# Dense products of the gate and the output projection listed behind the value projections in one sequence beside a recurrence, and the first chunk's operands in tiles of other pools

## The chip, the core and the metric

The kernel runs on one NeuronCore of a Trainium2 chip. The metric is device time in microseconds (us), the median of three executions. Next to the times there is one execution that was profiled; every duration below comes from that trace unless the text says otherwise. Engines: PE is the tensor engine (PEld its weight loads), DVE the vector engine, ACT the scalar engine, POOL GpSimd, SP the engine that only issues DMAs; ACT issues DMAs too.

## The reference, cut

A trunk of two layers on 512 positions of 1024 channels, each a mixer and a gated ConvFFN. The change lies in the second mixer, RWKV-7, whose core is a recurrence over positions, for 16 heads of 64 channels:

```python
def step(state, inp):
    r_t, w_t, k_t, v_t, a_t, b_t = inp
    sa = jnp.einsum('bhvk,bhk->bhv', state, a_t)
    state = (state * w_t[:, :, None, :]
             + sa[..., None] * b_t[:, :, None, :]
             + v_t[..., None] * k_t[:, :, None, :])
    y_t = jnp.einsum('bhvk,bhk->bhv', state, r_t)
...
r = xr @ w_r
k = xk @ w_k
v = xv @ w_v
g = jax.nn.sigmoid(xg @ g1) @ g2
...
return (y * g) @ w_o
```

## The kernel before, in words

Operands are stored transposed, channels on the 128 partitions and the 512 positions in the free dimension, so that a 1024-channel tensor is 8 tiles. Every dense product is done in float32r with both operands split into a high and a low part: three matmuls (lines 295, 296, 297, in the helper `mm3`) for each 128x128 block of weights. Such three are called a **set** below. Line 296 stands once in each set, so counting it counts sets.

The recurrence is done in chunks of 64 positions. First `pairs()` goes through the 8 tiles of channels (two heads each): decay, scaled operands, the products within a chunk. It writes three things to DRAM: `std` (for each group of four tiles and each chunk: the scaled operands and the masked products), `btd` and `vtd`. `invert(g)` inverts the 64x64 triangular blocks of group g (4 tiles): a long series of small DVE instructions on `pr` and `tt` (lines 964, 965), two DVE transposes (lines 970, 971), copies on ACT (975), and small matmuls (985, 988). Then `scan(g)` runs the 8 chunks of group g one after the other, 16 chunks in all, numbered 0 to 15 here (0 to 7 are group 0). One chunk is this chain:

1. PE: `us` and `e` from the chunk's operands `st` and values `vu` (lines 1105, 1109).
2. DVE copies `us` to `wt` (1107).
3. PE: the inverse `ti` times `wt` (1118).
4. DVE and ACT copy the result into `vu`, one head half each (1119, 1120).
5. PE: the new state from `vu` and `cbt` (1125), the rest of the output (1130).
6. DVE adds the decayed old state and writes it into `vu` of the next chunk (1128). ACT copies the output to `y` (1133).

Every second chunk is followed by `finish` (norm, transpose at line 1156, scale). `load(g, c)` fetches `st`, `vu` and `cbt` of a chunk through the SP queue (lines 1069, 1071, 1074), three buffers of each, in a pool `scan` that is opened when the pool of `pairs` is closed and takes its memory.

Beside this chain runs dense work, in generators that are advanced one step at a time: `projections()` (keys, then the values `v`; with each value tile four centring matmuls at line 784, one at 798, and the DMA of `vtd` at line 790), `gates()` (the product with g1, for each of eight channel tiles an operand made on ACT and DVE at lines 1010, 1011, 213, 214; then the product with g2 into `aux`, closed by line 1040), and `project()` (the output product `w_o`, added into `h` at line 1196). `weave` advances the chain and, after every step of it, the dense generator (`fill`) and the inversion (`side`) at the rates in the table `RATES`: the first number of an entry is steps of dense work for one step of the chain, the second a lag in steps, the third (0.5 where it is missing) steps of the inversion. The scheduler of the language then places each instruction in its engine's queue as early as its tiles and these marks allow; each engine works through its queue in order.

In the code before, `fill` is `projections()` alone until both `scan(0)` and the inversion of group 1 are emitted. What is left of it is then emitted at once, and only then `fill` becomes `gates()` followed by `project()`.

Of the kernel before, what the change touches and what calls it, by code (L numbers as in the profile page):

```python
# [12 lines left out]
F32 = mybir.dt.float32  # L13
# [7 lines left out]
P = 128  # L21
D = 1024
KT = 8
T = 512
# [4 lines left out]
GN_EPS = 64e-5  # L29
C1 = -0.5 * math.exp(-0.5)  # L30

RATES = ((1.9, 2), (1.9, 6, 2.2), (0.65, 2, 1), (0.9, 2), (2, 2), (0.7, 6, 2.2))
LEAD = 3
WB = 4
FIRST0, WAIT, STEPS = 1, 1, (2, 2, 2, 2, 2)
NKEY = 3
# [107 lines left out]
class Emit:  # L144
# [549 lines left out]
    def rwkv_main(self, r, ctx, gain):  # L694
# [10 lines left out]
        def tile_(shape, tag, bufs):  # L705
            return ep.tile(shape, F32, tag=tag, bufs=bufs, name=self.uid(tag))
# [354 lines left out]
        def load(g, c):  # L1061
            while 4 * g + 3 not in vdone:
                next(fill)
            ps = slice(4 * g, 4 * g + 4)
            st = tile_([P, 4 * 3 * P + P], "st", SCAN)
            bt, vu = tile_([P, 4, 2, C], "cbt", SCAN), tile_([P, 2, 4, C], "vu", SCAN)
            for hd in range(2):
                o = P * (1 - hd)
                nc.sync.dma_start(st[H[hd], o:o + 12 * P], std[g][c, H[hd]].rearrange("p i t -> p (i t)"))
# [9 lines left out]
        def scan(g, late=iter(())):  # L1079

            ih = [(i, hd) for i in range(4) for hd in range(2)]
            y = None

            for c in range(NCH):
                last = c == NCH - 1
                if (g, c) not in chunks:
                    load(g, c)
                st, bt, vu = chunks.pop((g, c))
                if (g, c) != (1, NCH - 1):
                    load(g + last, (c + 1) % NCH)  # L1090
                if c % 2 == 0:
                    y = tile_([P, 4, 2, C], "y", 3)
                us = self.acc("us").rearrange("p (a i f) -> p a i f", a=2, i=4)
                e = self.acc("e").rearrange("p (a i f) -> p a i f", a=2, i=4)

                def ar(i, hd, n):
                    o = P * (3 * i + 1 + hd) + n * C
                    return st[:, o:o + C]

                def pt(i, hd):  # L1100
                    o = P * (3 * i + 3 * (1 - hd)) + C
                    return st[H[hd], o:o + C]

                for i, hd in ih:
                    nc.tensor.matmul(us[H[hd], 0, i, :], ar(i, hd, 0), vu[:, hd, i, :], start=True, stop=True)
                wt = tile_([P, 4, C], "wt", 4)
                V.tensor_copy(wt, us[:, 0])
                for i, hd in ih:
                    nc.tensor.matmul(e[H[hd], 0, i, :], ar(i, hd, 1), vu[:, hd, i, :],
                                     start=i == 0, stop=False, skip_group_check=True)  # L1110
                if not last:
                    s0 = tile_([P, 4, C], "wt", 4)
                    for hd in range(2):
                        G.tensor_tensor(s0[H[hd]], vu[H[hd], hd], bc(gc[H[hd], 4 * g:4 * g + 4, c], C), ALU.mult)
                self.step(late)
                yield
                for i, hd in ih:
                    nc.tensor.matmul(us[H[hd], 1, i, :], ti[g][H[hd], i, c, :], wt[H[hd], i, :], start=True, stop=True)
# [55 lines left out]
        def project():  # L1174

            def load(g, m):
                return self.weights(A["wo"][m:m + 2, :, 512 * g:512 * g + 512].rearrange("m p c -> p m c"), lo_eng=G)

            ws = Ahead([lambda g=g, m=m: load(g, m) for g in range(2) for m in range(0, KT, 2)] + [self.prefetch])
            def back(m):  # L1180
                if m < KT:
                    nc.sync.dma_start(self.h[m], r.hd[m])

            for g in range(2):
                while g not in gated:
                    yield
                for m in range(KT):
                    if g == m == 0:
                        back(0)
                    if g == 0:  # L1190
                        back(m + 1)
                    if m % 2 == 0:
                        w = ws.take()
                    a = self.acc("mm")
                    yield from self.dense_steps(a, w, outs[g], c0=m % 2 * 512)
                    V.tensor_tensor(self.h[m], self.h[m], a, ALU.add)  # L1196
                    if g == 1:
                        self.absorb(m, gain)
# [7 lines left out]
        def until(gen, end):  # L1206
            for _ in gen:
                yield
                if end():
                    return  # L1210


        fill = projections()
        main = pairs()
        self.weave(until(main, lambda: 3 in done), None, fill, *RATES[0], ktiles=STEPS[0])
        inv = invert(0)
        for _ in take(inv, FIRST0):
            pass
        self.weave(until(main, lambda: KT - 2 in done), inv, fill, *RATES[1], ktiles=STEPS[1])
        self.weave(main, inv, fill, *RATES[5], ktiles=STEPS[1])  # L1220
        for _ in inv:
            pass
        ctx.close()
        ep = ctx.enter_context(tc.tile_pool(name="scan", bufs=1))
        inv = invert(1)
        gw = {}
        r.sg = [ep.tile([P, T], F32R, name=f"sg{i}") for i in range(3)]
        load(0, 0)
        next(inv)
        for _ in range(LEAD):  # L1230
            next(fill, None)
        self.weave(scan(0), inv, fill, *RATES[2], ktiles=STEPS[2])
        for _ in inv:
            pass
        for _ in fill:
            pass
        fill = itertools.chain(gates(), project())
        self.weave(scan(1, left.pop()), None, fill, *RATES[3], ktiles=STEPS[3])
        self.weave(left.pop(), None, fill, *RATES[4], ktiles=STEPS[4])
        for _ in fill:  # L1240
# [71 lines left out]
```

## Time and profile before

| | |
|---|---|
| median of 3 executions (lowest, highest) | 1329.78 us (1329.23, 1330.55) |
| the profiled execution's own time | 1334.18 us |
| its span, first to last instruction | 1332.4 us |
| PE busy | 1277.4 us (96%) |
| DVE busy | 853.5 us (64%) |
| ACT busy | 630.7 us (47%) |
| POOL busy | 142.1 us (11%) |
| mean granted clock of PE | 0.975 |

The profiled execution lies 4.40 us above the median. A matmul that waits in the pipeline counts as busy, so a busy PE is not PE at its peak; whether it works at full rate is seen in the granted clock and in the distance from one matmul's start to the next.

### The profile page before, as it was taken

Reading aid. Unit: us, or ns where it says so; the run is one execution under the profiler, and the core shown is the slowest. Engines: PE = TensorE matmul, PEld = TensorE weight load, DVE = VectorE, ACT = ScalarE, POOL = GpSimd, SP = SyncE. Lnnn points to the kernel's source line nnn. Section 1 sums busy time; section 2 is a strip of 40 time slices with the busy share of each in tenths; the row PEclk is TensorE's granted clock in tenths of the full one; section 3 lists DMA queues with packets and bytes.
Section 4 is the critical chain, followed back from the end, with each engine's and each line's share of the span. In section 5 each row is a group of like instructions: output and inputs, shape, how many; then the busy total and the mean of one; then the engine's idle time right before and its main releaser. Section 6 shows DMA issues by size and latency. Waiting matters only on the chain.

```text
span 1332.4 us, 19460 instructions
## 1 busy us (share of the span) xinstructions
PE 1277.4 (96%) x7578; PEld 1025.6 (77%) x7578; DVE 853.5 (64%) x1371; ACT 630.7 (47%) x1072; POOL 142.1 (11%) x148
## 2 busy tenths in 40 slices
PE   8999999999999999999999797799999999999996
PEld 6778888888888888677777666567888888888886
DVE  5565487887884444857788573576677777773223
ACT  5444365555553333656775443343554445452221
POOL 3100200000000001211210112123300000000001
PEclk9999999999999999999999887899999999999998
DMA  7232355555566653247778765683233333332322
GB/s 260 83 111 79 111 160 171 167 166 166 168 187 223 214 180 107 80 140 213 204 216 247 189 156 119 140 211 98 79 95 95 95 96 99 102 95 87 103 87 75
DMA packets 101100, 189.06 MB, mean 142 GB/s; under 512 B 16976, under 2 KB 48464, under 8 KB 101008
## 3 DMA queue, kind: packets, MB, share of 16 engines
q10 hardware_dynamic: 36592, 109.46, 27.1%
q1 hardware_dynamic: 64416, 78.36, 20.8%
q8 instruction: 59, 0.97, 0.3%
q14 instruction: 33, 0.27, 0.1%
HBM read 146.63 MB, written 41.16 MB: 141 GB/s over the span
## 4 chain that ended last, share of the span: by engine, by line
PE 76%; DVE 8%; DMA 4%; issue 3%; ACT 3%; POOL 1%; ACTq 0%; SPq 0%; DVEq 0%; POOLq 0%
PE mm L295 8%; PE mm L296 7%; PE mm L297 7%; PE aux L296 5%; PE aux L295 5%; PE aux L297 5%; PE us L295 5%; PE us L297 5%; PE us L296 5%; PE e L297 5%; PE e L296 5%; PE e L295 5%; DVE tt L965 1%; DVE pr L964 1%; PE e L1130 1%
## 5 line engine op out<-in xcount | busy, mean ns | idle before, releaser
L213 ACT CAST wh<-w 128x512 fp32r<-128x512 f32 x356 | 217.0, 612 | 386.4 <-PE mm L296 105.7
L214 DVE TENSOR_TENSOR wl<-w,wh 128x512 fp32r<-128x512 f32 x348 | 240.9, 693 | 180.0 <-ACT wh L213 178.6
L295 PE MATMUL mm<-mxh,wh 128*128 128x512 f32 (+1 forms) x384 | 157.4, 410 | 1.6 <-DVE h L1196 1.2
L297 PE MATMUL mm<-mxh,wl 128*128 128x512 f32 (+1 forms) x384 | 153.1, 399 | 0.4 <-DVE wl L214 0.3
L296 PE MATMUL mm<-mxl,wh 128*128 128x512 f32 (+1 forms) x384 | 152.2, 396 | 0.0
L322 POOL TENSOR_TENSOR ss<-ss,sq 128x512 f32<-128x512 f32 x30 | 41.9, 1397 | 776.5 <-issue 594.8
L518 ACT ACTIVATE cv<-z,par 128x512 f32<-128x512 f32 x88 | 71.7, 817 | 36.0 <-DVE z L516 35.9
L295 PEld LDWEIGHTS mm<-mxh,wh 128*128 128x128 f32 (+1 forms) x384 | 72.2, 188 | 20.6 <-issue 3.6
L297 PEld LDWEIGHTS mm<-mxh,wl 128*128 128x128 f32 (+1 forms) x384 | 72.3, 189 | 18.2 <-issue 0.9
L295 PE MATMUL e<-mxh,wh 128*128 128x512 f32 x216 | 84.5, 391 | 0.0
L296 PEld LDWEIGHTS mm<-mxl,wh 128*128 128x128 f32 (+1 forms) x384 | 72.6, 189 | 14.9 <-issue 0.7
L296 PE MATMUL e<-mxl,wh 128*128 128x512 f32 x216 | 84.1, 389 | 0.0
L297 PE MATMUL e<-mxh,wl 128*128 128x512 f32 x216 | 84.0, 389 | 0.0
L296 PE MATMUL aux<-mxl,wh 128*128 128x512 f32 x208 | 81.4, 391 | 2.7 <-POOL mxl L214 2.0
L295 PE MATMUL aux<-mxh,wh 128*128 128x512 f32 x208 | 81.5, 392 | 0.3 <-ACT mxh L213 0.3
L519 DVE SCALAR_TENSOR_TENSOR cv<-z,par,cv 128x512 f32<-128x512 f32 x88 | 66.1, 752 | 23.9 <-ACT cv L518 23.9
L295 PE MATMUL us<-mxh,wh 128*128 128x512 f32 x208 | 81.3, 391 | 0.0
L297 PE MATMUL aux<-mxh,wl 128*128 128x512 f32 x208 | 81.0, 389 | 0.0
L297 PE MATMUL us<-mxh,wl 128*128 128x512 f32 x208 | 81.0, 389 | 0.0
L296 PE MATMUL us<-mxl,wh 128*128 128x512 f32 x208 | 80.9, 389 | 0.0
L520 DVE SCALAR_TENSOR_TENSOR cv<-z,par,cv 128x512 f32<-128x512 f32 x88 | 66.0, 752 | 2.9
L296 PEld LDWEIGHTS aux<-mxl,wh 128*128 128x128 f32 x208 | 39.1, 188 | 12.3 <-POOL mxl L214 2.7
(1074 smaller groups left out, 2715.8 us busy)
## 6 DMA issues: line engine op xcount, KB each, us to landing
w<-in_wup ACTq DMA_DIRECT2D x88, 512.0 KB, 3.6
w<-in_wdn ACTq DMA_DIRECT2D x32, 512.0 KB, 3.6
st<-std SPq DMA_DIRECT2D x32, 384.0 KB, 5.8
std<-lq SPq DMA_DIRECT2D x32, 256.0 KB, 4.4
w<-in_wdn ACTq DMA_DIRECT2D x16, 384.0 KB, 3.2
w<-in_wsu ACTq DMA_DIRECT2D x8, 512.0 KB, 3.7
w<-in_wso ACTq DMA_DIRECT2D x8, 512.0 KB, 3.6
pw<-in_wk SPq DMA_DIRECT2D x16, 256.0 KB, 3.4
```

What stands on the lines that cost most here:

```text
L213: nc.scalar.copy(hi[r, :n], src)
L214: (lo_eng or nc.vector).tensor_tensor(lo[r, :n], src, hi[r, :n].bitcast(F32), ALU.subtract)
L295: mm(acc, wh, xh, start=first, stop=False)
L296: mm(acc, wh, xl, start=False, stop=False)
L297: mm(acc, wl, xh, start=False, stop=last)
L322: nc.gpsimd.tensor_tensor(self.ss, self.ss, self.sq, ALU.add)
L518: nc.scalar.activation(c, z[:, 2:], AF.Identity, scale=cw(2, i), bias=self.p("conv_b", l * 44 + i))
L519: nc.vector.scalar_tensor_tensor(c, z[:, 1:T + 1], cw(1, i), c, ALU.mult, ALU.add)
L520: nc.vector.scalar_tensor_tensor(c, z[:, 0:T], cw(0, i), c, ALU.mult, ALU.add)
L964: V.tensor_tensor(q, a, b, ALU.mult)
L965: V.tensor_tensor(tt[:, 0:nj, j + 1:32], tt[:, 0:nj, j + 1:32], q, ALU.add)
L1130: nc.tensor.matmul(e[H[hd], 0, i, :], pt(i, hd), vu[H[hd], hd, i, :], start=False, stop=True, skip_group_check=True)
```

## The change

Three things are edited.

- **The dense work is one sequence.** `fill` is `projections()`, `gates()` and `project()` chained, from the start. The emission of all that is left of `projections()` after `scan(0)` is gone. So gate work can stand beside the last chunks of group 0.
- **The rates.** `scan(0)` is woven at 0.62 in place of 0.65 steps, `scan(1)` at 0.85 in place of 0.9, and `LEAD`, the dense steps ahead of the first chunk, is 4 in place of 3.
- **The first chunk's load.** `load(0, 0)` is called before the last pair's products are woven instead of after the pools have changed. Its tiles therefore are not those of the pool `scan`: `st` are four tiles of the ring `mxh`/`mxl` (operands of dense products), `cbt` is the scratch tile `ss`, `vu` the scratch tile `rb`. It takes eight DMAs of 64x384 for `st` in place of two of 64x1536, so 11 DMAs in place of 5.

```diff
-RATES = ((1.9, 2), (1.9, 6, 2.2), (0.65, 2, 1), (0.9, 2), (2, 2), (0.7, 6, 2.2))
-LEAD = 3
+RATES = ((1.9, 2), (1.9, 6, 2.2), (0.62, 2, 1), (0.85, 2), (2, 2), (0.7, 6, 2.2))
+LEAD = 4
...
-            st = tile_([P, 4 * 3 * P + P], "st", SCAN)
-            bt, vu = tile_([P, 4, 2, C], "cbt", SCAN), tile_([P, 2, 4, C], "vu", SCAN)
-            for hd in range(2):
-                o = P * (1 - hd)
-                nc.sync.dma_start(st[H[hd], o:o + 12 * P], std[g][c, H[hd]].rearrange("p i t -> p (i t)"))
+            if g == c == 0:
+                st = [t for _ in range(2) for t in (self.xr.tile([P, T], F32, tag=tag, bufs=10, name=self.uid(tag))
+                                                    for tag in ("mxh", "mxl"))]
+                bt = scratch("ss").rearrange("p (i a f) -> p i a f", i=4, a=2)
+                vu = scratch("rb").rearrange("p (a i f) -> p a i f", a=2, i=4)
+                for i in range(4):
+                    for hd in range(2):
+                        o = P * (1 - hd)
+                        nc.sync.dma_start(st[i][H[hd], o:o + 3 * P], std[g][c, H[hd], i])
+            else:
+                t = tile_([P, 4 * 3 * P + P], "st", SCAN)
+                st = [t[:, 3 * P * i:3 * P * i + T] for i in range(4)]
...
-        fill = projections()
+        fill = itertools.chain(projections(), gates(), project())
+        gw = {}
...
+        load(0, 0)
         self.weave(main, inv, fill, *RATES[5], ktiles=STEPS[1])
...
-        load(0, 0)
         next(inv)
...
         for _ in inv:
             pass
-        for _ in fill:
-            pass
-        fill = itertools.chain(gates(), project())
         self.weave(scan(1, left.pop()), None, fill, *RATES[3], ktiles=STEPS[3])
```

Line numbers of the new code are 12 higher from `scan` on: 1117 for 1105, 1121 for 1109, 1119 for 1107, 1130 for 1118, 1131 and 1132 for 1119 and 1120, 1137 for 1125, 1142 for 1130, 1168 for 1156, 1081, 1083, 1086 for 1069, 1071, 1074.

What this does to the queues, at the three places on which the prediction rests. A row is line, operation, written tile, read tiles, shape, and a count where rows repeat; the number behind a tile's name tells its allocation.

**DVE at the start of `scan(0)`**, before. `pr`/`tt` are the inversion of group 1, `gwl` and `gw` the low parts of the g2 weights, `wt` is step 2 of chunk 0:

```order
L965 TENSOR_TENSOR tt_6678<-tt_6678,pr_6679 128x11x21
L214 TENSOR_TENSOR gwl_7641<-w_1431_7633,gwh_7640 128x512
L964 TENSOR_TENSOR pr_6679<-li_6677,tt_6678 128x240
L227 TENSOR_TENSOR gw_7636<-w_1431_7633,gw_7636 32x512
L965 TENSOR_TENSOR tt_6678<-tt_6678,pr_6679 128x12x20
L964 TENSOR_TENSOR pr_6679<-li_6677,tt_6678 128x247
L965 TENSOR_TENSOR tt_6678<-tt_6678,pr_6679 128x13x19
L1107 COPY wt_6741<-us_6731 128x256
```

and after:

```order
L965 TENSOR_TENSOR tt_6687<-tt_6687,pr_6688 128x8x24
L964 TENSOR_TENSOR pr_6688<-li_6686,tt_6687 128x207
L1119 COPY wt_6767<-us_6757 128x256
L965 TENSOR_TENSOR tt_6687<-tt_6687,pr_6688 128x9x23
L964 TENSOR_TENSOR pr_6688<-li_6686,tt_6687 128x220
L965 TENSOR_TENSOR tt_6687<-tt_6687,pr_6688 128x10x22
L1131 COPY rb_6572<-us_6757 64x256
L964 TENSOR_TENSOR pr_6688<-li_6686,tt_6687 128x231
L214 TENSOR_TENSOR gwl_7345<-w_1400_7337,gwh_7344 128x512
```

Chunk 0's first copy stands eleven rows earlier, behind the inversion's row of 128x207 and ahead of the g2 weights. On PE the same six dense matmuls stand ahead of chunk 0 in both.

**SP**, after. The rows with `ss` and `rb` are chunk 0's `cbt` and `vu`; the four with `std_4379` and `lq` are products of the last two pairs; `st_6748` begins chunk 1's load, at the place where chunk 0's load begins in the code before:

```order
L861 DMA std_4379<-ar_6245 64x8x128 x2
L1086 DMA ss_6571<-btd 128x512
L895 DMA std_4379<-lq_6270 64x4x256 x2
L790 DMA vtd<-vt_6302 128x8x64
L895 DMA std_4379<-lq_6329 64x4x256 x2
L906 DMA btd<-bt_6362 128x8x128
L790 DMA vtd<-vt_6443 128x8x64
L1083 DMA rb_6572<-vtd 64x256 x2
L895 DMA std_4379<-lq_6472 64x4x256 x2
L895 DMA std_4379<-lq_6596 64x4x256 x2
L906 DMA btd<-bt_6638 128x8x128
L790 DMA vtd<-vt_6696 128x8x64
```

The eight DMAs of chunk 0's `st` stand further up, among the writes of the fifth pair's products.

**PE in chunk 6**, before; lines 985 and 988 are the inversion of group 1, and no dense work stands in chunks 4 to 8:

```order
L1105 MATMUL us_7392<-vu_7228,st_7226 64x64 x7
L1109 MATMUL e_7393<-vu_7228,st_7226 64x64 x7
L988 MATMUL aux_7417<-li_7269,tt_7288 32x32 x32
L1118 MATMUL us_7392<-wt_7402,ti_4912 64x64 x8
L988 MATMUL aux_7468<-li_7269,tt_7288 32x32 x32
L1125 MATMUL us_7392<-vu_7228,cbt_7227 64x64 x8
L1130 MATMUL e_7393<-vu_7228,st_7226 64x64 x8
```

and after; `mm_7411` and `mm_7412` are the sums of the product with g1, `mxh_7416` and `mxl_7417` its first operand:

```order
L988 MATMUL aux_7460<-li_7284,tt_7297 32x32 x7
L295 MATMUL mm_7411<-mxh_7416,w_1404_7348 128x512
L295 MATMUL mm_7412<-mxh_7416,wh_7350 32x512
L988 MATMUL aux_7460<-li_7284,tt_7297 32x32 x6
L296 MATMUL mm_7411<-mxl_7417,w_1404_7348 128x512
L297 MATMUL mm_7411<-mxh_7416,w_1405_7349 128x512
L296 MATMUL mm_7412<-mxl_7417,wh_7350 32x512
L297 MATMUL mm_7412<-mxh_7416,wl_7351 32x512
L988 MATMUL aux_7460<-li_7284,tt_7297 32x32 x19
L1130 MATMUL us_7435<-wt_7445,ti_4912 64x64 x8
```

The gate's first two sets stand in chunk 6, where they stood in chunk 9 before. Counted over the queue (rows of line 296, full width), the sets stand like this:

| | chunks 0-3 | 4-9 | 10-14 | 15 and after, to the next stage |
|---|---|---|---|---|
| before | 14 | 4 | 29 | 51 |
| after | 14 | 14 | 22 | 48 |

The two DVE transposes of the inversion (lines 970, 971), which stand together in chunk 3 before, stand in chunk 4 after, with that chunk's `wt` copy between them.

More of the change, by code (lines that the diff above doesn't have):

```diff
@@ L1064, in load @@
             ps = slice(4 * g, 4 * g + 4)
-            st = tile_([P, 4 * 3 * P + P], "st", SCAN)
-            bt, vu = tile_([P, 4, 2, C], "cbt", SCAN), tile_([P, 2, 4, C], "vu", SCAN)
-            for hd in range(2):
-                o = P * (1 - hd)
-                nc.sync.dma_start(st[H[hd], o:o + 12 * P], std[g][c, H[hd]].rearrange("p i t -> p (i t)"))
+            if g == c == 0:
[10 more added lines that the diff above has]
+                st = [t[:, 3 * P * i:3 * P * i + T] for i in range(4)]
+                bt, vu = tile_([P, 4, 2, C], "cbt", SCAN), tile_([P, 2, 4, C], "vu", SCAN)
+                for hd in range(2):
+                    o = P * (1 - hd)
+                    nc.sync.dma_start(t[H[hd], o:o + 12 * P], std[g][c, H[hd]].rearrange("p i t -> p (i t)"))
             for hd in range(2):
@@ L1096, in ar @@
                 def ar(i, hd, n):
-                    o = P * (3 * i + 1 + hd) + n * C
-                    return st[:, o:o + C]
+                    o = P * (1 + hd) + n * C
+                    return st[i][:, o:o + C]
                 def pt(i, hd):
-                    o = P * (3 * i + 3 * (1 - hd)) + C
-                    return st[H[hd], o:o + C]
+                    o = P * 3 * (1 - hd) + C
+                    return st[i][H[hd], o:o + C]
                 for i, hd in ih:
@@ L1225, in rwkv_main @@
         inv = invert(1)
-        gw = {}
         r.sg = [ep.tile([P, T], F32R, name=f"sg{i}") for i in range(3)]
-        load(0, 0)
         next(inv)
```

## The prediction

> **What bounds the kernel now.** I read the page first (shares, granted clock), then the busy time by stages over the recurrence, then the order of time on PE, DVE, ACT and SP where PE is not full.
>
> ```profile
> PE 1277.4 (96%) x7578; PEld 1025.6 (77%) x7578; DVE 853.5 (64%) x1371; ACT 630.7 (47%) x1072; POOL 142.1 (11%) x148
> ...
> PEclk9999999999999999999999887899999999999998
> ```
>
> PE is the bound all along, except for the dip of its clock (a digit is a fortieth of the span, 33.3 us): that is the recurrence, and the change lies there alone. By stages (start:end, length, then busy us of PE, PEld, DVE, ACT, POOL with counts, granted clock, DMA share, GB/s):
>
> ```profile
> 752.90:770.30 17.40, 10.09 (x95) 8.02 (x94) 13.48 (x33) 4.32 (x10) 1.30 (x2) 0.64 1.04 263
> 770.30:800.30 30.00, 28.02 (x295) 19.75 (x294) 21.02 (x48) 12.77 (x24) 5.45 (x7) 0.90 0.60 141
> 800.30:808.20 7.90, 7.90 (x89) 6.18 (x88) 2.62 (x6) 2.95 (x8) 0.60 (x2) 0.67 0.01 2
> 808.20:816.50 8.30, 6.68 (x215) 5.77 (x213) 4.24 (x10) 3.46 (x9) 3.83 (x5) 1.00 0.96 223
> 816.50:831.00 14.50, 9.45 (x211) 8.63 (x209) 2.54 (x6) 4.17 (x8) 3.64 (x6) 0.59 0.64 138
> 831.00:836.10 5.10, 4.10 (x70) 3.52 (x68) 2.56 (x7) 1.10 (x3) 0.00 (x0) 0.82 0.77 176
> 836.10:840.40 4.30, 3.48 (x82) 2.88 (x80) 2.04 (x6) 1.73 (x4) 0.81 (x1) 1.00 1.00 220
> 840.40:858.30 17.90, 13.07 (x100) 7.86 (x99) 8.49 (x16) 4.93 (x9) 3.18 (x4) 0.71 0.44 97
> 858.30:867.40 9.10, 8.85 (x99) 5.57 (x98) 6.38 (x13) 5.42 (x10) 3.36 (x4) 1.00 0.61 132
> 900.70:908.80 8.10, 7.33 (x96) 5.13 (x95) 7.26 (x13) 3.39 (x9) 5.02 (x5) 1.00 0.54 168
> 858.30:914.10 55.80, 52.22 (x589) 36.30 (x590) 42.11 (x84) 27.38 (x55) 16.11 (x16) 1.00 0.68 177
> 914.10:953.50 39.40, 37.62 (x178) 30.36 (x174) 25.86 (x41) 17.90 (x34) 16.15 (x16) 1.00 0.26 81
> ```
>
> The rows are: chunk 0 with the wait ahead of it; chunks 1 to 3; chunks 4, 5, 6, 7, 8, 9; chunk 10; chunk 14; chunks 10 to 15; the dense rest. The same view of line 296 alone counts the sets:
>
> ```profile
> 858.30:867.40 9.10, 2.65 (x6) 0.88 (x6) 1.00 0.61 132
> 900.70:908.80 8.10, 1.91 (x5) 0.94 (x5) 1.00 0.54 168
> ```
>
> So a bare chunk at full clock takes 4.3 us (chunk 8), one with 6 sets 9.1, one with 5 sets 8.1. Dense matmuls start 0.22 to 0.23 us apart (752.29 and 752.51 in the next fence), a set costs 0.68 us; a loaded chunk is then 5.0 us and 0.68 for each set. Chunk 0 took 17.4 us with two sets, chunk 9 17.9 with four: waits and clock, not work.
>
> **The start of the chain, first term.** PE, DVE, ACT and SP in order of time (start, length, engine, line, form; in brackets the idle time before and its releaser); the last row, from the list of DMAs, ends with the median time to landing:
>
> ```profile
> 747.88 1.12 PE L798 MATMUL mm<-rt,wb 128*128 128x512 f32 x2 [0.36 <-ACT vt L789]
> 752.29 0.39 PE L296 MATMUL mm<-mxl,wh 128*128 128x512 f32 x1
> 752.51 0.39 PE L297 MATMUL mm<-mxh,wl 128*128 128x512 f32 x1
> 756.46 0.30 PE L1105 MATMUL us<-vu,st 128*64 128x64 f32 x2 [3.56 <-DMA w<-in_g]
> 761.60 1.12 PE L1118 MATMUL us<-wt,ti 64*64 64x64 f32 x16 [3.75 <-DVE wt L1107]
> ...
> 754.92 0.37 DVE L964 TENSOR_TENSOR pr<-li,tt 128x207 f32<-128x207 f32 x1
> 761.12 0.42 DVE L1107 COPY wt<-us 128x256 f32<-128x256 f32 x1
> ...
> 757.49 0.62 ACT L213 CAST gwh<-w 128x512 fp32r<-128x512 f32 x1 [5.17 <-DMA w<-in_g]
> ...
> 723.54 0.37 SPq L790 DMA_DIRECT2D vtd<-vt  x1
> 730.43 12.27 SPq L895 DMA_DIRECT2D std<-lq  x4
> ...
> 749.23 1.15 SPq L1069 DMA_DIRECT2D st<-std  x2
> ...
> vtd<-vt SPq DMA_DIRECT2D x3, 256.0 KB, 4.3
> ```
>
> PE's dense matmuls end at 752.9. Chunk 0's operands come at 756.5, because SP may start them only at 749.23, when the pairs' memory is free. Then DVE, in order, does the inversion and the g2 weights first, and copies `wt` at 761.12.
>
> After the change the operands are loaded beside the last pairs (SP's rows `ss`, `rb` and eight of `mxh`/`mxl`). The last of them, `rb`, needs the `vtd` write of the fourth value tile, which SP issued at 723.54; with 4.3 us to land that is 728, 25 us early. SP issues 11 DMAs in place of 5 at 0.58 us each (two took 1.15), 6.4 us in all, moved past the writes `std<-lq`, `btd` and `vtd`. It had nothing to issue from 723.9 to 730.4, and behind it wait only buffers of `lq` and `bt`; I cost that at nothing.
>
> The new course: line 1117 at 752.9. `wt` stands behind the row 128x207, which ended at 755.29: 755.3 to 755.7. Line 1130 until 756.4, three matmuls of line 784 and two sets until 758.2. The ACT half of `vu` still stands behind the cast `gwh`, which waits for its weights until 757.49: 758.8. Lines 1137 and 1142 until 760.1, line 798 (1.12) until 761. Chunk 0 takes 8 us in place of 17.4, with PE idle for 1.4 and 0.7 us.
>
> Chunks 1 to 3 keep their 12 sets. Of their 30.0 us the half clock took at most 3.0 (mean clock 0.90) and the transposes 1.66 (the wait at 793.93 below): 25.3 at best. But DVE was busy 34.5 us from 752.9 to 800.3 (13.48 + 21.02), of which only the transposes, 3.9, leave; 30.6 us of it in 33 would be a queue without gaps, though it waits for PE three times in each chunk. I take 28, nearer to what was.
>
> **Term A: 47.4 - 36 = 11.4 us.** Bounds: 2.7 more with 25.3, 5 to 7 less if the clock halves here all the same.
>
> **Chunks 4 to 9, second term.** What made them long:
>
> ```profile
> 789.87 1.96 DVE L970 STREAM_TRANSPOSE ix<-tt 128x1024 f32<-128x1024 f32 x1
> 791.68 1.93 DVE L971 STREAM_TRANSPOSE li<-tt 128x1024 f32<-128x1024 f32 x1
> 793.93 0.68 PE L1118 MATMUL us<-wt,ti 64*64 64x64 f32 x16 [1.66 <-DVE wt L1107]
> ...
> 791.87:795.29 3.42, 1.76 (x23) 1.37 (x22) 3.35 (x7) 1.64 (x2) 0.00 (x0) 1.00 0.84 179
> 795.29:805.53 10.24, 10.24 (x92) 7.81 (x91) 1.27 (x3) 5.12 (x9) 1.23 (x2) 0.50 0.00 1
> 757.74:771.39 13.65, 9.90 (x69) 7.72 (x68) 9.36 (x21) 4.08 (x10) 1.30 (x2) 0.50 1.06 273
> 754.33:757.74 3.41, 1.28 (x32) 1.27 (x32) 2.83 (x8) 0.25 (x1) 0.00 (x0) 1.00 1.06 284
> 750.91:754.33 3.42, 1.99 (x9) 1.31 (x7) 3.11 (x10) 0.82 (x2) 0.61 (x1) 1.00 0.89 212
> ...
> 819.69 0.37 PE L1109 MATMUL e<-vu,st 128*64 128x64 f32 x1 [2.84 <-issue]
> 827.47 1.49 PE L988 MATMUL aux<-li,tt 32*32 32x32 f32 x47 [2.21 <-issue]
> 844.09 0.80 PE L295 MATMUL mm<-mxh,w 128*128 128x512 f32 x1 [3.24 <-ACT mxh L213]
> ```
>
> The clock is granted in stretches of 3.41 us. Where PE was busy 1.28 or 1.76 us of 3.41 (38%, 51%), the next three or four stretches ran at half; where it was busy 1.99 (58%), the next did not. After the change:
> - chunk 4 has no set and both transposes (1.96, 1.93) ahead of its copies, and the first ACT copy of the inversion behind them: 10 us in place of 7.9, PE less than half busy. So the clock halves;
> - chunk 5 then runs at half: 11 in place of 8.3;
> - chunk 6 takes two sets into what was idle. Its first operand is a chain ACT, DVE, ACT like the one that cost 3.24 us at 844.09; the issue waits (2.84, 2.21) may stay in part. 10.8 in place of 14.5;
> - chunk 7 has four sets: 6.5 in place of 5.1; it has no line 1137. Chunk 8 two: 6.3 in place of 4.3;
> - chunk 9 has six and no first operand to wait for: 10 in place of 17.9.
>
> Sum 54.6, before 58.0. **Term B: 3.4 us.** Its bounds: 10 us if the clock stays full throughout, and a loss of 8 if two more first-operand waits come, each with a half stretch (2 x 3.24, and some 1.7).
>
> By the Trainium skill's page "TensorE: Matmul & The Clock Gate" (Why this matters for your kernels) only gaps over some 3 us bring the half rate back; here a gap of 1.66 us did, so the measurement decides. By that rule the sum would be the first rival's.
>
> **The sets moved away, third term.** Ten sets go into chunks 4 to 9 (4 before, 14 after): 7 from chunks 10 to 14, 3 from the dense rest. At full clock each is worth 0.68 us there. **Term C: 6.8 us.** The wait of chunk 12 for the gate's sigmoid, and ACT's for `w_o`, move along; I count them as equal. Rates and LEAD have no term of their own: they only set these counts.
>
> Sum: 11.4 + 3.4 + 6.8 = 21.6 us. From the profiled execution's 1334.18 us: 1312.6. It lies 4.4 us above the median of 1329.78, so the forecast for the median is 1308.
>
> **Rivals.**
> 1. The clock holds through chunk 4, because no single gap there fills a stretch of 3.41 us. Chunk 5 stays at 8.3 and chunk 6 gains 1: about 1304. Against it: 1.66 us were enough at 793.93. Chance 0.15.
> 2. The clock halves at chunk 0 all the same. My course leaves PE 1.4 us idle in the stretch 754.33 to 757.74, 59% busy, just above the 58% that passed. Price: up to half of 13.65 us, 5 to 6.8 on a PE-bound stretch: 1314. Chance 0.2.
> 3. The load was never the wait. The trace names the g2 weights (`w<-in_g`) as releaser at 756.46, and they come no earlier. If chunk 0 starts with them, only the order on DVE helps: A falls to some 2 us with the half clock kept, total 12: 1318; with a second such wait 1322. Against it: line 1105 reads no g2 weights. Chance 0.1.
> 4. Slower. PE is in order, and now each gate operand (ACT 1010, DVE 1011, ACT 213, DVE 214) stands ahead of the recurrence's own matmuls while ACT and DVE also carry the inversion. If each of the eight cost what the first did, 3.24 us, that is 25.9, more than 21.6; from 2.7 us each it decides. Against it is the sum of these waits below: 3.6 us in two. Chance 0.05.
>
> ```profile
> PE mm L295 <- ACT mxh L213: 3.6, 2, 3.2
> ```
>
> **How the numbers follow.** Forecast as summed 0.5, rivals 0.15, 0.2, 0.1, 0.05. The range takes in rivals 1 to 3 and the bounds of A and B: 1298 (A and B at their best lie 8.6 us below 1308, and 1.4 more) to 1322. Faster or slower means by over 0.2%, about 2.7 us, which is what a measurement of this kernel can tell from no change. Faster: the forecast, rivals 1 to 3 but for a tenth of the last: 0.92. Same 0.03; slower 0.05.
>
> **What would show it.** In the trace after: line 1117 within 1 us of the last dense matmul ahead of it, its `wt` some 3 us later, the first `vu` copy on ACT behind the cast `gwh`; no half clock in chunks 0 to 3; half clock from chunk 4 on; 14 sets in chunks 4 to 9 in under 56 us; chunk 9 near 10 us. A wait of over 2 us at each gate operand, or a half clock in chunk 0, would make the forecast wrong.

## The result, and the profile after

The changed kernel takes 1318.90 us (median of 4 runs, 1317.51 to 1320.53); the kernel before 1329.55 beside it. The ratio is 0.9884, with a 95% interval of 0.9842 to 0.9926: 10.65 us faster, about half of the 21.6 us forecast. Between the two profiled executions it is 13.65 us (1334.18 to 1320.53), since that of before lay 4.6 us above the 1329.55 and that of after 1.6 above its median.

From the page of the changed kernel, PE's busy time and its granted clock (a digit is 33.0 us):

```profile
PE 1275.4 (97%) x7578; PEld 1025.9 (78%) x7578; DVE 852.3 (65%) x1371; ACT 631.1 (48%) x1072; POOL 141.5 (11%) x148
...
PEclk9999999999999999999899896899999999999998
```

PE does the same work. Its clock has dips ahead of the recurrence now, and a deeper one in it (the 6). The busy time by stages, after (columns as in the prediction): everything ahead of chunk 0; chunks 0 to 3; chunks 4, 5, 6, 7, 8, 9; chunks 10 to 15; the dense rest.

```profile
0.00:758.10 758.10, 743.80 (x3984) 598.09 (x3984) 503.97 (x783) 395.23 (x673) 74.78 (x81) 0.98 0.54 166
758.10:791.80 33.70, 31.10 (x397) 22.73 (x396) 29.86 (x75) 13.49 (x31) 7.09 (x9) 1.00 0.95 224
791.80:800.90 9.10, 5.49 (x84) 4.03 (x83) 7.61 (x14) 4.64 (x8) 1.99 (x2) 0.79 0.71 164
800.90:811.30 10.40, 9.00 (x214) 8.00 (x213) 3.47 (x9) 5.70 (x10) 3.02 (x6) 0.66 0.55 122
811.30:824.60 13.30, 12.38 (x218) 9.63 (x214) 3.87 (x8) 5.89 (x10) 2.31 (x3) 0.50 0.36 86
824.60:832.30 7.70, 7.70 (x82) 5.51 (x81) 6.11 (x13) 3.69 (x7) 0.53 (x1) 0.79 0.65 155
832.30:839.20 6.90, 5.67 (x94) 3.62 (x90) 4.74 (x10) 4.56 (x10) 2.80 (x3) 1.00 0.82 183
839.20:853.20 14.00, 11.97 (x104) 7.11 (x103) 7.57 (x15) 3.85 (x7) 1.22 (x2) 0.88 0.33 79
853.20:902.50 49.30, 45.24 (x571) 33.46 (x572) 35.63 (x75) 21.82 (x46) 17.81 (x17) 1.00 0.77 211
902.50:938.30 35.80, 33.63 (x163) 27.27 (x160) 24.19 (x39) 16.54 (x31) 14.36 (x14) 1.00 0.23 70
```

Set beside the rows of before, with the time at half clock behind each (length x 2 x (1 - clock), from the clock's own steps of 3.41 us):

| us | before | after | difference | forecast |
|---|---|---|---|---|
| ahead of chunk 0 | 752.9 (10.2 half) | 758.1 (27.3 half) | +5.2 | 0 |
| chunks 0-3 | 47.4 (18.7) | 33.7 (0) | -13.7 | -11.4 |
| chunks 4-9 | 58.0 (29.1) | 61.4 (30.7) | +3.4 | -3.4 |
| chunks 10-15 | 55.8 (0) | 49.3 (0) | -6.5 | -4.8 |
| dense rest | 38.3 (0) | 35.8 (0) | -2.5 | -2.0 |

(The row of before for the dense rest ends 1.1 us later in the work than this one; 38.3 ends at the same matmul.) The start and the sets behind gave more than forecast. The middle gave a loss in place of a gain, and a stage that the change does not touch became longer.

The start, after: PE, DVE and ACT in order of time, and SP's issue of the last operand of chunk 0.

```profile
757.82 0.40 PE L297 MATMUL mm<-mxh,wl 128*128 128x512 f32 x1
758.15 0.34 PE L1117 MATMUL us<-rb,mxh 128*64 128x64 f32 x4
760.99 0.68 PE L1130 MATMUL us<-wt,ti 64*64 64x64 f32 x16 [1.27 <-DVE wt L1119]
764.48 0.69 PE L1137 MATMUL us<-rb,ss 128*64 128x64 f32 x16 [0.55 <-ACT rb L1132]
...
760.21 0.37 DVE L964 TENSOR_TENSOR pr<-li,tt 128x207 f32<-128x207 f32 x1
760.51 0.42 DVE L1119 COPY wt<-us 128x256 f32<-128x256 f32 x1
...
763.02 0.62 ACT L213 CAST gwh<-w 128x512 fp32r<-128x512 f32 x1 [5.18 <-DMA cbt<-btd]
764.06 0.37 ACT L1132 COPY rb<-us 64x256 f32<-64x256 f32 x1
...
734.38 1.14 SPq L1083 DMA_DIRECT2D rb<-vtd  x2
```

Line 1117 starts 0.33 us behind the last dense matmul (3.95 us before), and its operands were issued 24 us earlier. `wt` follows 2.4 us later, right behind the row 128x207. All as forecast.

### The profile page after: what moved, and what is told of

It reads as the page before. It is cut to its first block, busy times and chain, and to the rows that moved or that the text cites. A ratio compares the mean times of both kernels' runs of the same rounds, so it can differ in the third digit from the quotient of the medians.

```text
span 1318.7 us, 19468 instructions
## 1 busy us (share of the span) xinstructions
PE 1275.4 (97%) x7578; PEld 1025.9 (78%) x7578; DVE 852.3 (65%) x1371; ACT 631.1 (48%) x1072; POOL 141.5 (11%) x148
## 5 line engine op out<-in xcount | busy, mean ns | idle before, releaser
L519 DVE SCALAR_TENSOR_TENSOR cv<-z,par,cv 128x512 f32<-128x512 f32 x88 | 66.0, 751 | 23.9 <-ACT cv L518 23.9
L295 PEld LDWEIGHTS e<-mxh,wh 128*128 128x128 f32 x216 | 40.6, 188 | 8.9 <-issue 0.5
```

The costliest lines, as they stand in the source:

```text
L295: mm(acc, wh, xh, start=first, stop=False)
L519: nc.vector.scalar_tensor_tensor(c, z[:, 1:T + 1], cw(1, i), c, ALU.mult, ALU.add)
```

## The experiments

Single executions of one program spread by up to 18 us in these runs, and the mean clock explains nearly all of it. So each kernel is also given by two means over all its executions: the span times its mean clock, which is what the span would be at full clock, and what is left, the time lost to the half clock. The first hardly varies (standard deviation 0.5 to 2.8 us; the clock is given to 0.001, 1.3 us of a span); the second is uncertain by some 2 us in each row. Ratios are to the kernel before on the same chip. The row of before is that of the chip of the load alone, the sequence alone, the old rates and the changed kernel again; on the three other chips before had 1297.6 to 1298.2 us at full clock, but 34.4 to 35.0 us of loss in place of 32.3. So losses of different chips are set against before on the same chip.

| kernel | executions | median us | ratio (95%) | span x clock | lost to half clock |
|---|---|---|---|---|---|
| before | 17 | 1330.72 | 1 | 1298.0 | 32.3 |
| changed, first runs | 4 | 1318.90 | 0.9884 (0.9842-0.9926) | 1288.2 | 29.0 |
| changed, again | 6 | 1323.34 | 0.9920 (0.9890-0.9950) | 1288.7 | 30.8 |
| load alone | 5 | 1317.44 | 0.9895 (0.9874-0.9916) | 1292.2 | 24.0 |
| sequence alone | 12 | 1326.74 | 0.9964 (0.9941-0.9986) | 1292.5 | 33.3 |
| old rates | 6 | 1317.73 | 0.9895 (0.9864-0.9927) | 1288.9 | 27.2 |
| sets spread | 12 | 1327.43 | 0.9956 (0.9926-0.9986) | 1294.6 | 32.2 |
| changed, 31 extra matmuls | 6 | 1309.76 | 0.9824 (0.9790-0.9858) | 1293.0 | 16.2 |
| the same again | 6 | 1312.44 | 0.9833 (0.9798-0.9869) | 1293.8 | 17.3 |
| changed, 15 extra | 6 | 1314.30 | 0.9864 (0.9827-0.9902) | 1295.3 | 18.4 |
| load alone, 31 extra | 6 | 1323.47 | 0.9920 (0.9889-0.9951) | 1298.8 | 23.1 |
| load alone, 42 extra | 11 | 1325.08 | 0.9942 (0.9916-0.9968) | 1301.4 | 23.4 |
| before, 68 extra | 12 | 1336.89 | 1.0011 (0.9979-1.0044) | 1308.0 | 26.4 |

The change took 9.5 us out of the span at full clock (1298.0 to 1288.5) and 1.5 to 3.3 us out of the loss, which cannot be told from none. The forecast had counted on the loss itself to fall.

**The load alone.** Only the early load; two pieces of dense work and the old numbers.

```diff
...
-        fill = itertools.chain(projections(), gates(), project())
+        fill = projections()
...
+        for _ in fill:
+            pass
+        fill = itertools.chain(gates(), project())
         self.weave(scan(1, left.pop()), None, fill, *RATES[3], ktiles=STEPS[3])
```

> The kernel before with one part of the change: chunk 0's operands are loaded early into ring and scratch tiles; the dense work stays in two pieces, the rates and LEAD are the old ones. Theory 1 (the stage from the last dense matmul ahead of chunk 0 to the end of chunk 3 shrank from 47.4 to 33.7 us because of this load, and independently of the rest): that stage takes 33 to 37 us here and chunks 4 to 9 stay near 58, so the time is 11 to 14 us under before, about 1317. Theory 2 (the one sequence carries the gain, the load alone only moves the wait to the g2 weights): not more than 3 us under before, 1327 to 1330. Theory 3 (the early transfers cost the 5.2 us that the pairs' stage took longer): 6 to 9 us under before, with half-clock stretches ahead of chunk 0 at the same place.

1317.44 us: as fast as the whole change. Its chunks 0 to 3 and 4 to 9, and its longest waits of PE in the latter (total, times, longest):

```profile
751.70:786.30 34.60, 32.07 (x392) 23.13 (x392) 29.32 (x74) 13.73 (x32) 6.83 (x9) 1.00 0.96 229
786.30:841.20 54.90, 41.18 (x757) 32.26 (x756) 28.03 (x62) 22.85 (x43) 12.11 (x15) 0.81 0.60 136
...
PE mm L295 <- ACT mxh L213: 3.2, 1, 3.2
...
PE aux L988 <- issue: 1.8, 1, 1.8
```

The load alone takes 12.8 us out of chunks 0 to 3, although 16 sets stand in them in place of 14, so term A is the load's. Chunks 4 to 9, expected near 58, took 54.9 with 20.5 us of half clock in place of 29.1. Theories 2 and 3 fall. That chunk 0 starts right behind the dense work here also settles the prediction's third rival: the g2 weights named as releaser were not what it waited for.

**The sequence alone.** The new sequence and numbers; chunk 0's operands loaded late, into the recurrence's own tiles.

```diff
-            if g == c == 0:
+            if False:
...
-        load(0, 0)
         self.weave(main, inv, fill, *RATES[5], ktiles=STEPS[1])
...
+        load(0, 0)
         next(inv)
```

> The changed kernel without the early load: chunk 0's operands are loaded into the recurrence's own tiles when the pairs' memory is free, as before; one sequence of dense work, new rates. Theory 1 (sequence and load add up): chunk 0 waits for its load as before and keeps its half clock (chunks 0 to 3 some 45 to 48 us), the ten sets hidden in chunks 4 to 9 bring 9.0 us behind and cost 3.4 in the chunks, so 4 to 7 us under before: 1323 to 1326. Rival (they do not add up, since a late start shifts which chunks the half clock covers): below 1320 or not under before at all.

1326.74 us, 0.1 to 0.6% under before: near the first theory's 1323 to 1326. Its chunks 0 to 3 and 4 to 9, and the wait ahead of chunk 0:

```profile
755.70:800.60 44.90, 37.36 (x381) 26.58 (x380) 32.15 (x75) 15.67 (x31) 6.72 (x9) 0.77 0.80 187
800.60:858.50 57.90, 50.37 (x780) 36.03 (x779) 29.06 (x60) 24.98 (x49) 12.18 (x15) 0.79 0.56 129
...
758.42 0.45 PE L1117 MATMUL us<-vu,st 128*64 128x64 f32 x2 [2.71 <-DMA w<-in_g]
```

At full clock, load and sequence add up: 5.8 us (1298.0 to 1292.2) and 5.5 give 11.3, the whole change 9.5. On the loss they do not seem to: the load saves 8 us of it, and with the sequence 5 to 7 of these are back, each figure uncertain by some 3 us. The rival (that they do not add up) asked for a time below 1320 or no gain, and neither came.

**The old numbers**, with all the rest of the change.

```diff
-RATES = ((1.9, 2), (1.9, 6, 2.2), (0.62, 2, 1), (0.85, 2), (2, 2), (0.7, 6, 2.2))
-LEAD = 4
+RATES = ((1.9, 2), (1.9, 6, 2.2), (0.65, 2, 1), (0.9, 2), (2, 2), (0.7, 6, 2.2))
+LEAD = 3
```

> The changed kernel with the old numbers (0.65, 0.9, LEAD 3). Sixteen sets stand in chunks 0 to 3 in place of 14, none in chunk 6 in place of two, eight in chunks 7 and 8 in place of six. Theory 1 (the rates only set these counts, and a set costs 0.68 us wherever it is not hidden): within 3 us of the changed kernel, 1316 to 1322. Rival (the place of the first gate operand sets how far the half clock reaches): chunks 4 to 9 take 5 us more or less than 61.4, and the time follows.

1317.73 us, and 1288.9 at full clock against 1288.7: no difference that can be measured. Chunks 4 to 9 took 60.7 us, so the rival fell too. Set beside the load alone, which has the same numbers, this run is also the cleanest test of the sequence: 3.3 us less at full clock, 3.2 more loss, and the same ratio, 0.9895.

**The changed kernel again.**

> The changed kernel once more, unchanged. In its first profile the pairs' stage ran at half clock for 10.24 us (646.89 to 657.13) and for 3.4 us more, which the profile before did not, with the same instructions in the same order; the stage took 5.2 us longer. Theory 1 (chance: the 3.41 us stretches in which the clock is granted lie at another phase to the work in each execution): this profile shows the stretches in another place or not at all, and the recurrence begins near 753 to 755 in place of 758.1; single times spread over some 5 us. Rival (the early load causes them): half clock again near 647 to 657, and the recurrence begins near 758.

The profile looked like the rival: half clock at 648.9 to 659.1 and the recurrence's start at 760.2. The times look like chance: one program, 1314.62 to 1325.85, with the clock from 0.982 down to 0.972. One profile does not settle between the two. Chunks 0 to 3, 4 to 9 and 10 to 15 repeat the first profile but for one half stretch in chunk 0:

```profile
760.20:796.50 36.30, 32.47 (x395) 23.39 (x394) 29.95 (x75) 13.58 (x31) 7.09 (x9) 0.95 0.88 208
796.50:858.30 61.80, 52.49 (x780) 38.08 (x779) 33.58 (x67) 28.34 (x51) 12.02 (x14) 0.75 0.53 122
858.30:907.90 49.60, 45.31 (x573) 33.54 (x572) 35.55 (x74) 21.90 (x46) 17.67 (x16) 1.00 0.77 210
```

**Extra matmuls in chunks 4 to 7.** Nobody reads their result; they stand where PE waits for `wt` and `vu`.

```diff
+        WARM = {4: (10, 4), 5: (3, 4), 6: (3, 3), 7: (2, 2)}
+
+        def warm(g, c, j):
+            if g == 0 and c in WARM:
+                with tc.issue_after(self.last(mybir.EngineType.PE)):
+                    q = self.acc("us")
+                    for _ in range(WARM[c][j]):
+                        nc.tensor.matmul(q[:, 0:P], self.c("ident", P), self.c("ident", P), start=True, stop=True)
...
+                warm(g, c, 0)
                 self.step(late)
...
                 S.copy(vu[h1, 1], us[h1, 1])
+                warm(g, c, 1)
                 self.step(late)
```

> The changed kernel with 31 extra matmuls whose result nobody reads (128x128 f32 on constants, 0.29 us each, 8.9 us in all) in chunks 4 to 7, on PE behind lines 1117/1121 and 1130 of those chunks, where it waits for wt and vu: 14 in chunk 4, 7, 6 and 4 in the next. Theory 1 (the half clock is the price of an idle PE: chunks 4 to 9 ran 30.7 us of 61.4 at half rate, in both profiles of the changed kernel): the clock holds through chunk 7 or nearly, chunks 4 to 9 take 52 to 57 us although PE has more to do, and the time falls by 4 to 9 us. Rival (these chunks are bound by the chain through DVE and ACT, the clock only goes along): chunks 4 to 9 take 61 us or more, and the time rises by 0 to 9 us.

1309.76 us: more work and less time, 0.6 to 1.0% under the changed kernel by the ratios. Of the changed kernel, the stretch ahead of its first half clock in chunk 4 and the long one in chunks 5 to 7; of this one, chunks 4 to 9 as a whole and the stretch at the same place:

```profile
793.70:797.11 3.41, 1.01 (x17) 0.54 (x16) 3.38 (x3) 0.00 (x0) 0.00 (x0) 1.00 0.78 185
807.35:827.83 20.48, 19.56 (x348) 16.04 (x349) 7.88 (x15) 9.57 (x18) 4.67 (x7) 0.50 0.35 86
```

```profile
789.30:842.00 52.70, 49.56 (x841) 37.19 (x840) 33.68 (x67) 28.45 (x51) 12.61 (x14) 1.00 0.63 143
793.68:797.09 3.41, 2.38 (x12) 1.29 (x12) 2.70 (x5) 2.16 (x3) 1.06 (x1) 1.00 0.90 208
```

PE is busy 70% of that stretch in place of 30%, the clock stays at 1.00 throughout, and the six chunks take 52.7 us in place of 61.4. So the half clock is what they paid. Against before on the same chip, and beside the changed kernel again: 4.1 us more at full clock, 16.7 us less loss.

**The same with half of them.**

```diff
-        WARM = {4: (10, 4), 5: (3, 4), 6: (3, 3), 7: (2, 2)}
+        WARM = {4: (5, 2), 5: (2, 2), 6: (1, 1), 7: (1, 1)}
```

> The changed kernel with about half of the extra matmuls in chunks 4 to 7: 7 in chunk 4, 4 in chunk 5, 2 each in chunks 6 and 7, 15 in place of 31. If what counts is whether PE is busy over a share of a stretch of 3.41 us: in the changed kernel's chunk 4 the stretch ahead of the half clock was 31% busy and with 31 extra matmuls 70%; with half of them it is near 50%, where half rate has always followed in the traces so far; so half clock again in chunks 4 to 6, chunks 4 to 9 take 56 to 62 us, 1315 to 1322 in all. Rival (any work inside the gap is enough, since no gap then lasts over 2 us): the clock holds and chunks 4 to 9 take 50 to 53 us, 1306 to 1311.

1314.30 us, in between, so neither theory holds as written: chunks 4 to 9 take 57.5 us, within the first one's bounds, but the clock gives way in two single stretches only (6.8 us).

```profile
786.90:844.40 57.50, 49.01 (x809) 35.12 (x808) 34.04 (x67) 28.32 (x51) 12.35 (x14) 0.94 0.59 133
```

**Real sets in place of extra matmuls.** The changed kernel with 10, 8 and 2 sets in chunks 0-3, 4-6 and 7-8, where it had 14, 2 and 6.

```diff
-RATES = ((1.9, 2), (1.9, 6, 2.2), (0.62, 2, 1), (0.85, 2), (2, 2), (0.7, 6, 2.2))
-LEAD = 4
+RATES = ((1.9, 2), (1.9, 6, 2.2), (0.4, 2, 1), (1.0, 2), (2, 2), (0.7, 6, 2.2))
+LEAD = 2
```

> The changed kernel with other numbers in the table: scan(0) woven at 0.4 in place of 0.62, scan(1) at 1.0 in place of 0.85, LEAD 2 in place of 4. Chunks 0 to 3 take 10 sets in place of 14, chunks 4 and 5 two each in place of none, chunk 6 four in place of two, chunks 7 and 8 two in place of six, chunks 9 to 14 thirty-four in place of twenty-eight. Theory 1 (chunks 1 to 3 are bound by DVE, 22.55 us busy of 25.00, so sets are hidden there and taking some away gains little; sets in chunks 4 to 6 keep PE busy and the clock up): chunks 0 to 3 lose 0 to 3 us of their 33.7, the half clock of chunks 4 to 9 falls from 30.7 to under 20 us, and the time is 3 to 8 us under the changed kernel. Rival (two sets are 1.36 us of a stretch of 3.41 and do not lift its share over a half where DVE holds the chain up): the clock halves as before, and the time stays within 3 us, or chunks 1 to 3 now fall to half clock too and it rises.

1327.43 us, slower than the changed kernel. Chunk 1, left without sets, shows why it is no clean test. The window is that chunk; the rows are DVE's, ACT's and PE's:

```profile
762.60:776.40 13.80, 6.83 (x90) 5.86 (x89) 8.57 (x20) 3.56 (x8) 1.31 (x2) 0.75 0.82 183
...
768.27 0.69 DVE L214 TENSOR_TENSOR gwl<-w,gwh 128x512 fp32r<-128x512 f32 x1 [4.53 <-ACT gwh L213]
769.75 0.43 DVE L1119 COPY wt<-us 128x256 f32<-128x256 f32 x1
...
767.62 0.62 ACT L213 CAST gwh<-w 128x512 fp32r<-128x512 f32 x1 [5.29 <-DMA w<-in_g]
...
770.23 1.12 PE L1130 MATMUL us<-wt,ti 64*64 64x64 f32 x16 [6.38 <-DVE wt L1119]
```

The g2 weights now stand on DVE ahead of chunk 1's `wt` and are late, so PE waits 6.38 us and the clock falls. Chunks 0 to 3 took 36.4 us. Chunks 4 to 9, with 16 sets in place of 14, took 64.9, more than in the changed kernel, although their half clock fell from 30.7 to 20.5 us; PE had two issue waits there, 2.7 and 2.6 us. The second half of the rival came out (half clock in chunks 1 to 3 and a longer time), but by a wait for the g2 weights that it did not name, so the question of this run, sets against extra matmuls, stays open.

**The kernel before again**, for its trace.

> The kernel before once more, unchanged, for its trace. If half-clock stretches ahead of the recurrence come by chance in any execution, whatever the kernel, this profile may show some besides the one at 727 to 737 us, where its first profile showed none, and the recurrence then begins later than 752.9 by half their length; the half clock in chunk 0 and in chunks 4 to 9 comes back (12.6 and 29.1 us), since the same waits leave PE idle there. If the pairs' stretches belong to the changed kernel, there are none here.

1330.60 us. The half clock came back in chunks 0 to 3 (17.1 us) and 4 to 9 (23.9 in place of 29.1); ahead of the recurrence there was one stretch of 3.4 us that its first profile did not have, and the start was at 753.6.

**The kernel before with extra matmuls**: the same function, numbers {0: (12, 3, 13), 4: (6, 4), 5: (5, 5), 6: (6, 6), 7: (4, 4)}, the third of chunk 0 ahead of its first row. (An entry for chunk 8 here and in the run with 42 does nothing, since group 0 ends with chunk 7.)

> The kernel before, with nothing of the change, but with extra matmuls whose result nobody reads (128x128 f32, 0.25 us from start to start): 28 in chunk 0 (13 ahead of its first row, while its load is under way; 12 behind it; 3 behind line 1118) and 40 in chunks 4 to 7. Theory 1 (most of what the late load and the empty chunks cost is half clock, not waiting): the time falls although the load is as late as before, by half of the 18.7 us of half clock in chunks 0 to 3 and of most of the 29.1 in chunks 4 to 9, 12 to 20 us less than before: 1312 to 1322. Rival (the waits themselves cost, the clock only goes along): within 5 us of before.

No gain: 1336.89 us, with a ratio of 1.0011, as the rival had it. Some half clock went (a loss of 26.4 us against 35.0 on this chip), and chunks 0 to 3 fell from 47.4 to 40.4 us; but they began 3.6 us later, since 13 of the matmuls stand ahead of the last two sets, and the span at full clock grew by 10 us. The first theory was wrong in taking the filled waits as free. Chunks 4 to 9, and a wait in chunk 6 with no releaser in the profile (line 1086 there holds the extra matmuls, and the trace lists each of them as two):

```profile
796.90:855.80 58.90, 49.89 (x839) 40.08 (x838) 22.32 (x50) 19.32 (x40) 12.67 (x16) 0.86 0.55 127
...
818.49 1.45 PE L1086 MATMUL us<-cst 128*128 128x128 f32 x10 [3.42 <-issue]
```

**The load alone with extra matmuls**, 42 of them first ({4: (8, 4), 5: (5, 5), 6: (6, 6), 7: (4, 4)}), then the 31, beside the changed kernel with 31 on one chip.

> The early load alone (two pieces of dense work, old rates) with 42 extra matmuls in chunks 4 to 7. It is compared with the changed kernel that had 31 of them (median 1309.8): what is left between the two is what the one sequence is worth where the clock holds in both. Theory 1 (span times mean clock was 1292.2 us for the load alone and 1288.5 with the sequence; the half clock hid the difference): 2 to 6 us more than 1309.8, 1312 to 1316. Rival (sets moved into chunks 4 to 9 cost there what they save behind): the same within 2 us or less.

> The early load alone (two pieces of dense work, old rates) with the same 31 extra matmuls in the same places as the first kernel that had them (14, 7, 6, 4 in chunks 4 to 7), where the run with 42 (12, 10, 12, 8) came out at 1325. It stands beside that first kernel on the same chip. Theory 1 (the 42 stood on the chain in chunks 5 to 7, which hold no sets and in which PE waits little; fewer of them cost less): 3 to 8 us under 1325, 1317 to 1322, no better than the load alone without any. Theory 2 (extra work pays only where sets stretch the chunks, so one sequence and a busy PE gain together): it stays 6 to 12 us above the kernel with sequence and extra matmuls. Rival (31 matmuls hold the clock here as well): 1309 to 1314.

> The changed kernel with the 31 extra matmuls once more, unchanged. If its gain was no accident of one chip: no half clock in chunks 4 to 9, these take 52 to 54 us, and the ratio to the kernel before is again 0.979 to 0.986.

With 42, 1325.08; with 31, 1323.47; without any, 1317.44 on another chip. By the ratios (0.9920 with 31, 0.9895 without) there is no gain. Against before on the same chip, the 31 cost 7.0 us more at full clock and save 3.6 us of loss. Both theories of the first text missed, since the clock did not hold in the load alone. The first theory of the second text asked for a larger fall from 42 to 31 than the 1.6 us found; its second one, that sequence and extra work gain together, came out, with 11.0 us between the two kernels on one chip (1323.47 - 1312.44). The window is chunks 4 to 9 of the load alone with 31, and the rows its longest waits of PE there; then the same window of the changed kernel with 31, again:

```profile
789.20:847.80 58.60, 48.64 (x819) 38.65 (x818) 28.36 (x62) 22.94 (x43) 12.13 (x15) 0.83 0.55 127
...
PE mm L295 <- ACT mxh L213: 3.6, 2, 3.2
...
PE aux L988 <- issue: 2.4, 1, 2.4
```

```profile
796.00:848.80 52.80, 49.71 (x841) 37.23 (x840) 33.79 (x67) 28.44 (x51) 12.65 (x14) 1.00 0.63 143
```

In the old order two waits that no extra matmul fills are left, an issue wait in chunk 6 and the first gate operand's 3.2 us in chunk 9, and the clock halves at each (from 815.0 and from 832.0 us). In the changed kernel with 31 neither is there. So the one sequence gains nothing over the load as it stands (1318.9 and 1323.3 against 1317.4), but with the clock held it does. The changed kernel with 31 extra matmuls is the fastest of all, 1.7 to 1.8% under before in both runs; the second of them bore out the third text in full.

## Why the prediction was half right

- **Term A (11.4 us forecast, 13.7 measured; load alone 12.8): right in mechanism.** Chunk 0 took 8.7 us (forecast 8), with waits of 1.27 and 0.55 us (1.4 and 0.7). The mis-sized step is chunks 1 to 3: I took 28 us against a bound of 25.3, thinking DVE could not be filled further. It took 25.0, and DVE was busy 22.55 of them.
- **Term B (3.4 us gain forecast, 3.4 us loss measured): the step that failed.** Chunks 4, 5, 7 and 8 came near (9.1, 10.4, 7.7, 6.9 us; forecast 10, 11, 6.5, 6.3). Chunk 6 was put at 10.8 and took 13.3, chunk 9 at 10 and took 14.0. I let the half clock end with chunk 5, after the three or four stretches that it had lasted before. It came back within chunk 5 for 20.5 us, six stretches, to chunk 7, although PE counted as busy for 19.56 us of them, and again in chunk 9. The waits I feared for the gate operands stayed small (in all 2.1 us in three), so what made chunk 6 long was the clock. With the clock held, chunk 6 took 10.1 and chunk 9 11.5. In chunk 9 the 3.4 us at half clock are 1.7 of the 4.0 us too much; PE also waits there 1.6 us for `vu` and 1.4 for dense operands.
- **Term C (6.8 us forecast, 9.0 measured): right in mechanism.** Seven sets left chunks 10 to 15 (4.8 us of PE, 6.5 measured), three the dense rest (2.0; 2.5). What gave the other 2.2 us was not looked for.
- **The pairs' stage, assumed unchanged: 5.2 us more in the profile.** It is the clock again. The same stretch of 3.41 us in the changed kernel and in the one with 31 extra matmuls, which has the same instructions in the same order up to chunk 4, each with what followed:

```profile
643.48:646.89 3.41, 2.45 (x17) 1.40 (x17) 1.96 (x5) 2.65 (x6) 0.40 (x1) 1.00 0.88 213
646.89:657.13 10.24, 10.24 (x56) 8.57 (x57) 5.06 (x10) 6.59 (x12) 1.40 (x2) 0.50 0.46 122
```

```profile
643.48:646.89 3.41, 2.46 (x17) 1.66 (x14) 2.32 (x5) 2.59 (x7) 1.31 (x1) 1.00 0.83 226
646.89:650.31 3.42, 3.42 (x36) 2.71 (x36) 2.26 (x6) 2.74 (x6) 0.00 (x0) 1.00 0.81 207
```

Busy 72% in both; one then ran at half for 10.24 us, the other did not, and its second profile had such a stretch again, at 650.8. So the order of the program does not fix the outcome there. Whether the early load makes it likelier is not settled: 5 of 10 profiles with it had that stretch, none of 4 without, and all half clock ahead of chunk 0 came to 10.2 to 13.7 us without the load, and to 17.1 to 30.7 in those five.

- **The rivals.** The first (the clock holds through chunk 4; 1304) and the fourth (3.24 us for each gate operand) did not happen, nor did the half clock in chunk 0 but for one stretch in the second profile. The third was refuted by the load alone. None of them named what happened: the half clock that left chunks 0 to 3 (18.7 us) stood elsewhere, 17.1 us more of it ahead of chunk 0 and 1.6 more in chunks 4 to 9.
- **The sum.** 13.7 - 3.4 + 9.0 - 5.2 = 14.1 us by stages, 13.65 between the profiled executions, 10.65 between the medians. That the time lies inside the range given, 1298 to 1322, is in part luck. The upper bound was the price of the third rival, which did not happen; the half clock in the pairs' stage had no term at all; and what A and C gave more (4.5 us) covered part of what B and that stage took (12.0). When the kernel was run again, four of six executions lay above 1322. Three slips in the working change nothing of this: A and B at their best lie 2.7 + 6.6 = 9.3 us below 1308, not 8.6; two more first-operand waits at 3.24 us and 1.7 for one or both half stretches leave B a loss of 4.8 or 6.5, not 8; and the chances named for "faster" add up to 0.94, not 0.92.

## What to carry to other kernels

Split a measured gain into span times clock and what the clock lost, over several executions: an edit that removes waits shows in the first at once, and may give it all back in the second. Work moved into a stage that runs at half clock is not hidden there by being beside idle time; look first whether it lifts PE's share of a 3.41 us stretch above about two thirds, where half clock seldom followed in these traces, unless the work there was small matmuls. Extra matmuls in the waits can pay, as they did in the changed kernel; in the load alone and in the kernel before, where other waits stayed, they did not.

## What the runs showed of the hardware

- The granted clock changes on a grid of 3.41 us whose place against the program differs between executions; within a profile all half stretches start on one grid (its place in the span, taken in steps of 3.413 us, lies between 0.14 and 3.39 us in 14 profiles). The Trainium skill, page "TensorE: Matmul & The Clock Gate" (Part 1: The HAM clock gate), says of this window that it is free-running and does not reset when a kernel starts. The traces agree.
- The share of PE's busy time in a stretch goes with what follows it, but does not settle it. Counted over the full-clock stretches of the 14 profiles from 500 us to 1250 us: under 55% busy, 42 of 45 were followed by half clock; 55 to 65%, 18 of 38; over 65%, 23 of 2820. The same part of the Trainium skill's page lets the half rate follow a window that was idle; here it followed windows that were half full, so the measurement decides. Of the 23, seven were 71 to 74% busy, but the other sixteen 86 to 100%. In each of these sixteen stand the eight matmuls of line 836 (128x2) and 12 to 32 of line 902 (64x64), and of all full-clock stretches with so many of both, 16 of 19 were followed by half clock. So a stretch that the profile shows as busy with small matmuls can lose the clock too. One of the sixteen, in the changed kernel, with the stretch behind it:

```profile
667.37:670.78 3.41, 3.27 (x42) 3.01 (x41) 0.71 (x4) 2.94 (x7) 0.00 (x0) 1.00 0.88 230
670.78:674.20 3.42, 3.42 (x19) 2.42 (x20) 2.29 (x5) 1.83 (x4) 0.92 (x2) 0.50 0.74 233
```

- Nor did a busy PE end the half clock at once: of 145 half-clock stretches in the same part of the profiles in which PE was at least 95% busy, 62 were followed by another. Why was not tried.
- PE has waits that nothing in the profile releases ("issue", the long ones 1.7 to 3.4 us) in chunk 6, where some 210 small matmuls stand in a row. The changed kernel, whose chunk 6 has two sets among them, has none, but the sequence alone, with the same two sets, has one of 1.7, and the run with the sets spread has two, of 2.7 and 2.6, in chunks 4 to 9. Their cause was not tried.
